# Wide hi products in the feed-forward: one matmul of 512 columns in place of two of 256

## The chip, the core and the metric

The kernel runs on one core of a Trainium2 chip. The metric is device time in microseconds (us) of one execution. Before the change the median of three runs is 1216.08 us (1213.23 to 1216.94).

## The reference: what is computed

A trunk of two layers on one sequence of 256 tokens with 1024 features, all in float32. Each layer has three sub-layers: a SwiGLU feed-forward, a token mixer, and a second feed-forward. So there are four feed-forwards. Layer 0 mixes by sparse attention beside a gated delta rule, layer 1 by latent attention. Every sub-layer modulates its input by the conditioning vector c and ends in a residual and a LayerNorm:

```python
def swiglu(u, w_gate, w_up, w_down):
    return (jax.nn.silu(u @ w_gate) * (u @ w_up)) @ w_down

def adaln_sublayer(x, m, f, ln_g, ln_b):
    shift, scale, gate = m[:, None, 0], m[:, None, 1], m[:, None, 2]
    y = f(x * (1 + scale) + shift)
    return layer_norm(DEEPNORM_ALPHA * x + (1 + gate) * y, ln_g, ln_b)
```

The inner width of a feed-forward is 2816. The modulation m is c (after a SiLU) times a matrix of 1024 rows per sub-layer, plus a bias.

## The kernel before, in words

**Products in three parts.** To reach float32 accuracy with the matmul type f32r, each operand is split into a hi part (rounded, a cast on ScalarE, ACT) and a lo part (the rest, a subtraction on VectorE, DVE, or on GpSimd, POOL): `split`, lines 257 to 259. A product of two split operands is three matmuls into the same PSUM bank: hi by hi, hi by lo, lo by hi (`mm3`, lines 261 to 266). TensorE (PE) loads the first operand as weights and streams the second as moving columns.

**A feed-forward** (`ffn`, line 412) goes over 22 tiles of 128 inner columns, in 11 chunks of two tiles. The input u stands transposed in `uT` [128, 2 (hi, lo), 8 row tiles, 256 tokens]. For each chunk the kernel loads and splits 256 columns of w_gate and w_up (`load`, line 439; the split tiles are named g and u, three buffers each) and the rows of w_down (`load_down`, line 456; tile hd). Each chunk but the first then fills four PSUM banks, gate and up of two tiles: for each of the 8 row tiles k an `mm3` with the weights hl[:, 0, k], hl[:, 1, k] and moving columns u[:, 0, k] (hi) or u[:, 1, k] (lo), 256 columns each (lines 529 to 535). So a bank takes 24 matmuls and uses 256 of its 512 columns. The tag `gu` has four banks, and the modulation sums use the same tag.

Behind each pair of banks ACT takes Silu of the gate bank into the tile sg (line 548), DVE multiplies the up bank by sg (line 551), and the result h is split (ACT, then DVE, line 553). The products with w_down follow one chunk later: for every tile four `mm3` with 512 moving columns into four banks of tag `acc` (`down`, lines 429 to 435, called at line 567); the last five tiles come at the end, bank by bank (lines 568 to 570).

The first chunk differs: in the first feed-forward it follows an order written by hand (lines 496 to 499), in the three others it is computed by rows of tokens (`by_rows`, line 463; `turned`, line 476).

**Beside it** runs the modulation of later sub-layers: `pace` (line 55) is called for each tile and takes steps of `mod_gen`, each of which loads 128 rows of a matrix (tile wd) and adds them, scaled, to macc on DVE (line 225). When eight steps are done, PE sums macc over its partitions, by four matmuls with ones in two halves (line 180) or by eight transposes (line 138); these stand in PE's queue behind the products of a chunk. In the first feed-forward the set-up of masks and positions runs beside the chunks as well.

**Order.** The engines run their queues in order. The tile framework writes the queues and the semaphores; `behind(mark)` has what is traced inside it come behind the marked instruction on its engine. `load(c)` of a chunk is behind the split of h of chunk c - 2 (line 522). SP's queue issues the loads in their order and waits where a buffer is not free: three buffers w8 for gate and up, three wd for w_down and the modulation. Memory pools of one sub-layer take over the space of the one before, and tiles there wait for the old ones.

Of the kernel before, what the change touches and what calls it, by code (L numbers as in the profile page):

```python
# [15 lines left out]
ALU = mybir.AluOpType  # L16
# [14 lines left out]
HYBRID_LATE, LATENT_LATE = (1,), (5,)  # of these rows, the second block's products come last  # L31


class Trunk:
# [20 lines left out]
    def pace(self, part):  # L55
        """runs the modulation up to its share of what this sub-layer takes of it"""
        goal = self.base + math.ceil((self.goal - self.base) * min(part, 1.0))
        while self.count < goal:
            self.count += next(self.bg)
        if part > 1.0:  # L60
            self.need(self.si, 2)
            if self.si + 1 < len(self.subs):
                self.need(self.si + 1, 0)

# [18 lines left out]
    def setup_bias(self):  # L83
        """the biases of shift and scale, as columns"""
# [25 lines left out]
    def behind(self, *marks):  # L110
        """what is traced here is issued behind the marked instructions of the same engines"""
# [9 lines left out]
    def warm(self, a):  # L121
        """keeps the PE array's clock up while nothing else can run on it"""
# [3 lines left out]
    def preload(self, func, after):  # L126
        """has the table of an activation function loaded behind what makes the tile after"""
        self.nc.scalar.activation(self.tl(self.const, [P, 1], "d"), after[:, 0:1], func)

# [1 line left out]
    def mod_cols(self, acc):  # L131
        """sum of acc over its partitions, [column % 128, column // 128]"""
# [9 lines left out]
    def mod_cols0(self, acc, c, use=None):  # L142
        """the same by products with c, which start earlier; use: takes two columns at a time"""
# [31 lines left out]
    def mod_gate(self, si, acc, G):  # L175
        """G holds the bias"""
# [8 lines left out]
    def mod_gen(self):  # L185
        """(c @ mod_w + mod_b) of every sub-layer, in the order of use; partition sums come last; yields tiles loaded"""
# [82 lines left out]
    def make_u(self, si, n, blocks):  # L269
        """n [P, NB, D] tokens on partitions -> uT = n * A + B, hi and lo [P, 2, KD, S]; blocks: one or all of them"""  # L270
# [57 lines left out]
    def residual(self):  # L328
        """x <- alpha * (n * g + b), in place of n; in four steps"""
# [16 lines left out]
    def epilogue(self, si, acc, last):  # L346
        """x holds alpha * x; acc the four banks of f(u); leaves the normalised rows in x, or the output."""
# [63 lines left out]
    def ffn(self, l, f, first):  # L411
        """first: the tiles of w_gate and w_up come first in the pool's memory, or those of w_down"""
# [6 lines left out]
        with ExitStack() as es:  # L419
# [18 lines left out]

            def load(c, tok):
# [23 lines left out]
            def by_rows(hls):  # L463
                """h of two tiles of columns, with tokens on partitions first: a block can run without the other"""
# [11 lines left out]
            def turned(pts):  # L476
                """the rest of by_rows"""
# [16 lines left out]
            else:  # L494
                # the products of the first chunk as their parts come: 0 hi hi, 1 hi lo, 2 lo hi; a pair of rows; gate, up
# [24 lines left out]
            for c in range(NC):  # L520
# [6 lines left out]
                else:  # L527
                    pts = {(s, g): self.bank("gu", (P, S)) for s in r2 for g in r2}
                    if c:
                        for s in r2:  # L530
                            for g in r2:
                                for k in range(KD):
                                    hl = hls[s, g]
                                    self.mm3(pts[s, g], hl[:, 0, k], hl[:, 1, k], u[:, 0, k], u[:, 1, k],
                                             k == 0, k == KD - 1)
# [8 lines left out]
                for s in r2:  # L544
                    i = 2 * c + s
                    if not tok:
                        sg = self.tl(hp, [P, S], "sg", bufs=2)
                        nc.scalar.activation(sg, pts[s, 0], AF.Silu)  # L548
                        if i == NT - 1 and f == 0:
                            self.preload(AF.Tanh, sg)  # L550
                        nc.vector.tensor_tensor(out=sg, in0=pts[s, 1], in1=sg, op=ALU.mult)
# [86 lines left out]
    def setup_rope(self):  # L638
        """cos and signed sin of the rotary angles: [frequency, token] and [token, frequency]"""
# [22 lines left out]
        # rows: 0-63 one, 64-95 cos, 96-127 signed sin  # L662
# [12 lines left out]
    def proj_t(self, pool, w, c0, n, use, engs=(None,)):  # L675
        """u @ w[:, c0 + o : c0 + o + 128] for o = 0, 128, ... < n, transposed: [columns, tokens]."""
# [17 lines left out]
    def tok_load(self, pool, w, c0, W):  # L694
        """the rows of w[:, c0 : c0 + W], split, in tiles of as many as fit"""
# [11 lines left out]
    def proj_tok(self, hls, W, by_block):  # L707
        """u @ the rows hls, with tokens on partitions; a bank for each block; by_block: one block after the other"""
# [17 lines left out]
    def attend(self, pool, q, k, v, bias, escale, po, i, sums, tags):  # L726
        """one head: q, k transposed, v [P, NB, 64]; exp(escale * (logits + bias) - max) @ v into po[:, :, i], its sums
        into sums[:, :, i]"""
# [21 lines left out]
    def attended(self, pool, po, sums, mix, k0):  # L750
        """divides the four heads of po by their sums; transposed into rows k0, k0 + 1 of mix"""
# [751 lines left out]
```

## Time and profile before

| what | us |
|---|---|
| three runs | 1213.23, 1216.08, 1216.94 |
| span of the profiled execution (first to last instruction) | 1212.3 |
| its own time beside the span | not listed; the runs are 0.9 to 4.6 longer than this span |
| busy PE, DVE, ACT, POOL | 1135.4, 905.5, 547.6, 255.4 |

The page of the profile gives busy time and instruction counts of each engine; groups of instructions by line, operation and tile; the waits between engines; and the instructions in order of time. PE's durations overlap, since matmuls are pipelined: the distance between two start times is the price of a matmul, not its duration. PEld is the weight load, beside PE. The four feed-forwards' chunks of two tiles start at about 46, 492, 694 and 1024 us.

### The profile page before, as it was taken

Reading aid. Unit: us, or ns where it says so; the run is one execution under the profiler, and the core shown is the slowest. Engines: PE = TensorE matmul, PEld = TensorE weight load, DVE = VectorE, ACT = ScalarE, POOL = GpSimd, SP = SyncE. Lnnn points to the kernel's source line nnn. Section 1 sums busy time; section 2 is a strip of 40 time slices with the busy share of each in tenths; the row PEclk is TensorE's granted clock in tenths of the full one; section 3 lists DMA queues with packets and bytes.
Section 4 is the critical chain, followed back from the end, with each engine's and each line's share of the span. In section 5 each row is a group of like instructions: output and inputs, shape, how many; then the busy total and the mean of one; then the engine's idle time right before and its main releaser. Section 6 shows DMA issues by size and latency. Waiting matters only on the chain.

```text
span 1212.3 us, 19687 instructions
## 1 busy us (share of the span) xinstructions
PE 1135.4 (94%) x7783; PEld 1035.5 (85%) x7783; DVE 905.5 (75%) x1376; ACT 547.6 (45%) x959; POOL 255.4 (21%) x186
## 2 busy tenths in 40 slices
PE   4998999999899998999999899899989998999997
PEld 3897999788787887989999889799978878899995
DVE  6699777698985677878885888778788438866545
ACT  0644444456433445533543543334456556544430
POOL 0631000224731452320000322000221234300001
PEclk9999999999999999999999999999999998999999
DMA  9779999454310586788997488889725135876620
GB/s 352 249 260 345 303 319 303 145 165 123 98 36 5 188 274 212 243 291 297 325 307 238 139 283 284 269 297 302 266 79 168 66 105 180 295 250 189 215 72 35
DMA packets 155334, 259.76 MB, mean 214 GB/s; under 512 B 8813, under 2 KB 117354, under 8 KB 155242
## 3 DMA queue, kind: packets, MB, share of 16 engines
q1 hardware_dynamic: 155050, 258.45, 63.9%
q8 instruction: 61, 1.00, 0.3%
q14 instruction: 31, 0.25, 0.1%
q10 hardware_dynamic: 192, 0.05, 0.0%
HBM read 257.43 MB, written 1.05 MB: 213 GB/s over the span
## 4 chain that ended last, share of the span: by engine, by line
PE 51%; DVE 22%; DMA 13%; ACT 5%; issue 5%; POOL 3%; SPq 0%; POOLq 0%; DVEq 0%; ACTq 0%
PE gu L265 8%; PE gu L264 8%; PE gu L263 7%; DMA wd<-ffn_w_down 7%; PE acc L265 6%; PE acc L263 6%; PE acc L264 6%; DVE macc L225 3%; DMA wd<-mod_w 3%; DMA w<-ffn_w_up 2%; DVE g L259 2%; POOL hd L259 2%; PE gu L732 2%; DVE u L259 2%; ACT hd L258 1%
## 5 line engine op out<-in xcount | busy, mean ns | idle before, releaser
L225 DVE SCALAR_TENSOR_TENSOR macc<-wd,csT,macc 128x1024 f32<-128x1024 f32 x112 | 169.0, 1509 | 27.1 <-DMA wd<-mod_w 26.5
L263 PE MATMUL gu<-uT,g 128*128 128x256 f32 x640 | 181.1, 283 | 1.4 <-ACT sg L548 1.4
L265 PE MATMUL gu<-uT,g 128*128 128x256 f32 x640 | 181.2, 283 | 1.2 <-DVE g L259 1.2
L265 PE MATMUL gu<-uT,u 128*128 128x256 f32 x640 | 181.2, 283 | 1.0 <-DVE u L259 1.0
L263 PE MATMUL gu<-uT,u 128*128 128x256 f32 x640 | 181.1, 283 | 0.0
L264 PE MATMUL gu<-uT,u 128*128 128x256 f32 x640 | 181.1, 283 | 0.0
L264 PE MATMUL gu<-uT,g 128*128 128x256 f32 x640 | 181.1, 283 | 0.0
L258 ACT CAST hd<-wd 128x1024 fp32r<-128x1024 f32 x88 | 92.2, 1049 | 136.8 <-DMA wd<-ffn_w_down 118.9
L263 PE MATMUL acc<-hd,h 128*128 128x512 f32 x352 | 141.3, 401 | 1.5 <-ACT h L258 1.5
L265 PE MATMUL acc<-hd,h 128*128 128x512 f32 x352 | 137.6, 391 | 1.1 <-DVE h L259 1.1
L264 PE MATMUL acc<-hd,h 128*128 128x512 f32 x352 | 137.7, 391 | 0.0
L259 DVE TENSOR_TENSOR g<-w,g 128x1024 fp32r<-128x1024 f32 x86 | 118.9, 1386 | 22.8 <-ACT g L258 22.3
L263 PEld LDWEIGHTS gu<-uT,g 128*128 128x128 f32 x640 | 122.7, 192 | 3.2 <-ACT sg L548 1.8
L265 PEld LDWEIGHTS gu<-uT,g 128*128 128x128 f32 x640 | 122.7, 192 | 1.6 <-DVE g L259 1.6
L264 PEld LDWEIGHTS gu<-uT,g 128*128 128x128 f32 x640 | 122.7, 192 | 1.4
L265 PEld LDWEIGHTS gu<-uT,u 128*128 128x128 f32 x640 | 122.9, 192 | 1.2 <-DVE u L259 1.2
L263 PEld LDWEIGHTS gu<-uT,u 128*128 128x128 f32 x640 | 122.9, 192 | 0.0
L264 PEld LDWEIGHTS gu<-uT,u 128*128 128x128 f32 x640 | 122.9, 192 | 0.0
L259 DVE TENSOR_TENSOR u<-w,u 128x1024 fp32r<-128x1024 f32 x81 | 104.1, 1290 | 24.5 <-ACT u L258 24.3
L258 ACT CAST u<-w 128x1024 fp32r<-128x1024 f32 (+1 forms) x89 | 91.6, 1039 | 62.7 <-DMA w<-ffn_w_up 51.9
L259 POOL TENSOR_TENSOR hd<-wd,hd 128x1024 fp32r<-128x1024 f32 x32 | 86.6, 2712 | 141.6 <-ACT hd L258 141.6
L259 POOL TENSOR_TENSOR hl<-w,hl 128x1024 fp32r<-128x1024 f32 x28 | 72.5, 2602 | 202.2 <-ACT hl L258 201.7
(392 smaller groups left out, 2495.2 us busy)
## 6 DMA issues: line engine op xcount, KB each, us to landing
wd<-mod_w SPq DMA_DIRECT2D x130, 512.0 KB, 4.8
wd<-ffn_w_down SPq DMA_DIRECT2D x88, 512.0 KB, 4.6
w<-ffn_w_gate SPq DMA_DIRECT2D x43, 1024.0 KB, 8.3
w<-ffn_w_up SPq DMA_DIRECT2D x43, 1024.0 KB, 6.9
w<-hyb_w_in SPq DMA_DIRECT2D x16, 1024.0 KB, 6.1
w<-mod_w SPq DMA_DIRECT2D x7, 1024.0 KB, 7.5
w<-hyb_w_out SPq DMA_DIRECT2D x4, 1024.0 KB, 4.9
w<-mla_w_out SPq DMA_DIRECT2D x4, 1024.0 KB, 5.4
```

Source lines behind the costliest of these rows:

```text
L225: step = nc.vector.scalar_tensor_tensor(acc, w, c, acc, ALU.mult, ALU.add)
L258: i = self.nc.scalar.copy(hi, src)
L259: return i, (eng or self.nc.vector).tensor_tensor(out=lo, in0=src, in1=hi.bitcast(F32), op=ALU.subtract)
L263: nc.tensor.matmul(out, lh, rh, start=first, stop=False)
L264: nc.tensor.matmul(out, lh, rl, start=False, stop=False)
L265: self.last_mm = nc.tensor.matmul(out, ll, rh, start=False, stop=last)
L732: nc.tensor.matmul(pt[:, b * S : (b + 1) * S], q[:, b * P : (b + 1) * P], k, start=True, stop=True)
```

## The change

In each chunk but the first, a bank holds [2, 256] columns. For each row tile the products of the hi weights with u-hi and u-lo become one matmul with 512 moving columns, u-hi's sum in the first half and u-lo's in the second. All eight of these come first; the eight products of the lo weights with u-hi then add into the first half. The two halves are added behind it: ACT copies the second half to SBUF, DVE adds the first half to it. Silu and the product of gate and up then read the sums in SBUF. The up sums have a new tile su of two buffers.

```diff
+    def mm_wide(self, out, hl, u):
+
+        nc = self.nc
+        for k in range(KD):
+            nc.tensor.matmul(out.rearrange("p a b -> p (a b)"), hl[:, 0, k], u[:, :, k], start=k == 0, stop=False)
+        for k in range(KD):
+            nc.tensor.matmul(out[:, 0], hl[:, 1, k], u[:, 0, k], start=False, stop=k == KD - 1)
...
+            def whole(pt, out):
+
+                nc.scalar.copy(out, pt[:, 1])
+                nc.vector.tensor_tensor(out=out, in0=pt[:, 0], in1=out, op=ALU.add)
+                return out
...
-                    pts = {(s, g): self.bank("gu", (P, S)) for s in r2 for g in r2}
+                    pts = {(s, g): self.bank("gu", (P, 2, S) if c else (P, S)) for s in r2 for g in r2}
                     if c:
                         for s in r2:
                             for g in r2:
-                                for k in range(KD):
-                                    hl = hls[s, g]
-                                    self.mm3(pts[s, g], hl[:, 0, k], hl[:, 1, k], u[:, 0, k], u[:, 1, k],
-                                             k == 0, k == KD - 1)
+                                self.mm_wide(pts[s, g], hls[s, g], u)
...
                         sg = self.tl(hp, [P, S], "sg", bufs=2)
-                        nc.scalar.activation(sg, pts[s, 0], AF.Silu)
+                        pg, pu = pts[s, 0], pts[s, 1]
+                        if c:
+                            pg, pu = whole(pg, sg), whole(pu, self.tl(hp, [P, S], "su", bufs=2))
+                        nc.scalar.activation(sg, pg, AF.Silu)
                         if i == NT - 1 and f == 0:
                             self.preload(AF.Tanh, sg)
-                        nc.vector.tensor_tensor(out=sg, in0=pts[s, 1], in1=sg, op=ALU.mult)
+                        nc.vector.tensor_tensor(out=sg, in0=pu, in1=sg, op=ALU.mult)
```

## Rows read from the trace of the kernel before

**Rows 1.** The page's part 1: span, busy time of each engine, share, instructions.

```profile
span 1212.3 us, 19687 instructions
PE 1135.4 (94%) x7783; PEld 1035.5 (85%) x7783; DVE 905.5 (75%) x1376; ACT 547.6 (45%) x959; POOL 255.4 (21%) x186
```

**Rows 2.** The page's groups, first and last of six: count, busy, mean ns, idle.

```profile
L263 PE MATMUL gu<-uT,g 128*128 128x256 f32 x640 | 181.1, 283 | 1.4 <-ACT sg L548 1.4
...
L264 PE MATMUL gu<-uT,g 128*128 128x256 f32 x640 | 181.1, 283 | 0.0
```

**Rows 3.** Timeline of PE, 599.8 to 604.2 us: start, duration, instruction.

```profile
599.87 0.39 PE L263 MATMUL acc<-hd,h 128*128 128x512 f32 x1
...
601.23 0.28 PE L263 MATMUL gu<-uT,g 128*128 128x256 f32 x1
...
604.11 0.28 PE L263 MATMUL gu<-uT,u 128*128 128x256 f32 x1
```

**Rows 4.** Busy time by stretch, late parts: stretch, length, engines, clock, DMA share, GB/s.

```profile
125.00:237.00 112.00, 110.19 (x769) 102.98 (x768) 82.80 (x107) 46.59 (x66) 6.00 (x4) 1.00 0.80 265
570.00:667.00 97.00, 97.00 (x690) 91.09 (x689) 72.87 (x90) 41.89 (x59) 1.24 (x1) 1.00 0.86 292
766.00:875.00 109.00, 109.00 (x750) 101.40 (x749) 84.71 (x103) 43.91 (x64) 3.63 (x2) 0.99 0.85 283
```

The busy times in these rows are of PE, PEld, DVE, ACT and POOL, in this order.

**Rows 5.** The same view, stretches in the opening of the feed-forwards.

```profile
60.00:99.00 39.00, 33.78 (x239) 31.54 (x237) 37.94 (x62) 13.74 (x18) 15.65 (x40) 1.00 0.83 277
487.00:511.00 24.00, 22.90 (x171) 21.78 (x171) 23.69 (x23) 13.35 (x20) 8.12 (x3) 1.00 0.72 246
511.00:570.00 59.00, 56.95 (x395) 52.41 (x394) 44.00 (x45) 23.56 (x33) 11.99 (x5) 1.00 0.88 293
550.00:560.00 10.00, 9.56 (x80) 9.39 (x80) 9.46 (x12) 4.47 (x6) 0.00 (x0) 1.00 0.91 305
687.00:714.00 27.00, 25.35 (x192) 23.92 (x191) 26.07 (x27) 15.35 (x23) 8.07 (x3) 1.00 0.65 216
1020.00:1038.00 18.00, 17.43 (x141) 16.71 (x139) 17.45 (x11) 12.83 (x17) 11.97 (x5) 1.00 0.71 230
```

**Rows 6.** Timeline of PE: instructions that waited, in brackets how long and for what.

```profile
98.99 1.17 PE L180 MATMUL gu<-macc,one 128*128 128x512 f32 x1 [4.19 <-DVE macc L225]
...
559.90 0.30 PE L138 MATMUL gu<-ident,macc 128*128 128x128 f32 x1 [0.44 <-DVE macc L225]
...
761.49 0.33 PE L138 MATMUL gu<-ident,macc 128*128 128x128 f32 x1 [0.90 <-ACT sg L548]
...
765.16 0.47 PE L138 MATMUL gu<-ident,macc 128*128 128x128 f32 x1 [3.01 <-DVE sg L551]
...
1038.75 0.50 PE L265 MATMUL acc<-hd,h 128*128 128x512 f32 x1 [1.07 <-DVE h L259]
```

**Rows 7.** Waits of PE, whole span: for whom, us in total, times, longest.

```profile
PE gu L282 <- DVE x L407: 6.0, 2, 3.6
...
PE gu L265 <- DVE g L259: 1.2, 1, 1.2
...
PE gu L265 <- DVE u L259: 1.0, 1, 1.0
```

**Rows 8.** Instructions on tile gu: ns min/median/max, first and last start, form.

```profile
L548 ACT ACTIVATE sg<-gu x82: 365/379/402, 40.6 to 1185.3; 128x256 f32<-128x256 f32 x82
L551 DVE TENSOR_TENSOR sg<-gu,sg x82: 407/419/427, 42.3 to 1188.2; 128x256 f32<-128x256 f32 x82
```

**Rows 9.** Timeline of DVE around 99 us.

```profile
98.76 0.42 DVE L551 TENSOR_TENSOR sg<-gu,sg 128x256 f32<-128x256 f32 x1
99.09 0.42 DVE L634 TENSOR_TENSOR nd<-nd,mneg 128x256 f32<-128x256 f32 x1
```

**Rows 10.** Busy time, sum over 46:99, 487:560, 687:762 and 1020:1039 us.

```profile
sum 220.00, PE 207.32 PEld 195.71 DVE 188.05 ACT 99.94 POOL 76.54; mean PE 51.83 PEld 48.93 DVE 47.01 ACT 24.98 POOL 19.13
```

**Rows 11.** Timeline of DVE in the second feed-forward, at 552 us.

```profile
552.18 0.42 DVE L259 TENSOR_TENSOR h<-sg,h 128x256 fp32r<-128x256 f32 x1 [0.47 <-ACT h L258]
```

## The prediction, made before the run

> **What bounds the kernel now.** I read the busy times first, then stretches, then the waits. The page's first part [rows 1] shows TensorE (PE) busy for 94% of the span, VectorE (DVE) 75%, ScalarE (ACT) 45%: PE is the engine to shorten, but the change pays for it on DVE, so DVE is the engine to watch. The cost groups [rows 2] show the six groups that the change touches: 640 matmuls each, 3840 in all, 40 chunks of 96 (ten chunks in each of four feed-forwards). Their 283 ns is a modelled duration that overlaps the next one, so the price is read from start times [rows 3]: six products with 512 columns start between 599.87 and 601.23 us, 227 ns apart; then the 24 products of one gate bank, 256 columns each, take 601.23 to 604.11 us, 120 ns apart. In a feed-forward's later part PE does not pause [rows 4]: in 570 to 667 us it is busy 97.00 of 97.00 us and in 766 to 875 us 109.00 of 109.00, with DVE at 72.87 and 84.71. There every nanosecond off PE is time off the kernel. In the opening of each feed-forward it is the other way round [rows 5]: DVE is busy 37.94 of 39 us (60 to 99), 23.69 of 24 (487 to 511), 26.07 of 27 (687 to 714) and 17.45 of 18 (1020 to 1038), and PE waits there for what DVE delivers. The places where it does are few [rows 6]: the first product of a modulation sum, which stands in PE's queue behind a chunk's products, waits 4.19 us at 98.99, 0.44 at 559.90, 0.90 and 3.01 at 761.49 and 765.16; and a lo product waits 1.07 for h at 1038.75. I call these the pins: what PE saves between the feed-forward's start and its last pin only makes the wait at the pin longer.
>
> **The change, part by part.** *Products.* In a bank 16 of the 24 products of 256 columns become 8 of 512. Before: 24 x 120 = 2880 ns. After: 8 x 227 + 8 x 120 = 2776 ns. That is 104 ns a bank, 0.416 us a chunk, and 160 banks give 16.6 us. The trace has no 512-column product whose moving operand lies in two runs (u-hi and u-lo are apart in memory). Bounds: 227 ns, the contiguous 512 [rows 3], and 240 ns, twice the 256, where nothing is saved; I take 227, the row with the same count of columns. The streaming itself is not shortened, only the part of each pitch that does not grow with the columns: 2 x 120 - 227 = 13 ns per pair.
>
> The Trainium skill, "TensorE: Matmul & The Clock Gate", section "Back-to-back issue gap", gives a warm gap of columns / 2.4 GHz plus 2.5 ns. An estimate from it would save 2.5 ns a pair, 3.2 us in 1280 pairs. The rows here disagree with it by some 11 ns at either width, so the sum above stays.
>
> *Order of the products.* The eight hi products now come first, so a bank can start when ACT's cast of its weights has ended, and DVE's subtraction (the lo part) is needed 8 x 0.227 = 1.8 us later. The two waits of PE for that subtraction, 1.2 and 1.0 us [rows 7], should go. Both lie ahead of the pin at 98.99, so what they free is late there instead: I count nothing.
>
> *ACT.* 160 copies of 128x256 out of PSUM; the nearest row is the Silu from the same kind of bank, 379 ns [rows 8]: 61 us in all. In the late stretches ACT is busy 46.59 of 112 us [rows 4], so the work itself costs nothing. The copy of the up half waits for PE to finish that bank, and the next weights' casts and the Silu are queued behind it; ACT already holds there today, since its next step, the cast of h, waits for DVE's product, which waits for the same bank. Without that cover it would cost its own 0.38 us.
>
> *DVE.* 160 additions of 128x256, one operand in PSUM; the row is the product of gate and up, the same form, 419 ns [rows 8], and where nothing holds it the next one starts 0.33 us after it [rows 9]. That is 4 x 0.42 = 1.7 us a chunk, 67 us in all. In 570 to 667 us there are 97 / 17.0 = 5.7 chunks (17.0 us is 96 x 0.120 + 24 x 0.227), so DVE goes from 72.87 to 82.5 of 97 us: hidden [rows 4]. In the full stretches it is not hidden, and I price the shift at the last pin of each feed-forward at 0.33 us an addition:
> - First, pin at 98.99: eight additions lie ahead of it in the full stretch (two of chunk 1, four of chunk 2, two of chunk 3): 2.7 us. The gain of chunks 1 to 3, 1.2 us, is lost in the wait. Together 3.9.
> - Second, pin at 559.90: DVE is busy 9.46 of the 10 us before [rows 5], with the two additions of chunk 4's first tile in them: 0.7, and the gain of chunks 1 to 4 lost, 1.7: 2.4. The additions of the chunks before fall into DVE's idle time (44.00 busy of 59 us from 511 to 570 [rows 5]).
> - Third, pins at 761.49 and 765.16: a gate bank is now freed by DVE's addition, not by ACT's Silu, and DVE stands in a run of weights there: 0.7, and 1.7 lost: 2.4.
> - Fourth, pin at 1038.75: four additions, 1.3, and 0.4 lost: 1.7.
>
> Bounds of this part: below, 5.0 us (the lost gain alone, 1.2 + 1.7 + 1.7 + 0.4, all additions behind the pins); above, every addition ahead of a pin at 419 ns plus the copy that it waits for, which is the second rival.
>
> *PSUM banks and memory.* The four banks are the same size. A bank is freed one ACT copy and one DVE addition after its last product, 0.8 us plus queueing; it is written again after the other three banks and 24 products of 512 columns, 3 x 2.8 + 5.4 = 13.8 us later: nothing, except at the pins counted above. The new tile su takes 2 KB of each partition, so pools of the next sub-layers lie elsewhere and may wait for other tiles. Bounds: 0 and 3.6 us, the longest wait of PE at such a border today (for the normalised rows, L407) [rows 7]; I take 0, as no row shows a wait on memory there.
>
> **The sum.** 16.6 - (3.9 + 2.4 + 2.4 + 1.7) = 16.6 - 10.4 = 6.2 us less. The profiled execution has a span of 1212.3 us [rows 1], 3.8 under the median of the runs, 1216.08; the saving is taken from the span and carried to the median: 1206.1 and **1209.9 us**.
>
> **The rivals.** (1) *The additions are free.* DVE's queue puts them where it waits for loads, and since PE frees buffers sooner, the loads that feed the pins come sooner too: 16.6 us, 1199.5. For it: DVE has 25% idle over the span [rows 1] and the lo parts gain 1.8 us of leeway. Against: at 60 to 99 us there is 1.06 us idle for eight additions. Chance 0.18.
>
> (2) *DVE becomes the bound, slower.* The place is DVE's in-order queue between a feed-forward's start and its last pin. Each addition there holds the queue until ACT's copy has ended, 0.38 + 0.42 = 0.80 us a bank, 3.2 a chunk; up to the pins there are 3 + 4 + 4 + 1 = 12 chunks, 38.4 us. It shows as PE idle where DVE is full, 39 + 24 + 10 + 27 + 18 = 118 us [rows 5] of the 220 us up to the pins [rows 10], 54%: 20.6 us. After the pins 28 chunks gain 11.6. Net 9.0 slower, 1225.1. It decides where an addition is put ahead of a weight split whose PE consumer is waiting; for it, DVE waits 0.47 us for ACT's cast of h today, the same kind of hold [rows 11]. Against: the next weights' splits can be queued between copy and addition. Chance 0.18.
>
> (3) *The wide product saves nothing*, at 240 ns because of its two runs: then only the additions at the pins count, 2.7 + 0.7 + 0.7 + 1.3 = 5.4 slower, 1221.5. Chance 0.07. The gap rule of the Trainium skill's page "TensorE: Matmul & The Clock Gate" ("Back-to-back issue gap") lies near this case; the 120 and 227 ns of this trace speak against it.
>
> (4) *The memory moves.* Borders cost up to 3.6 us; at one or two of three borders the gain of 6.2 is mostly gone: about 1215. Chance 0.12.
>
> **How the numbers follow.** A measurement of this kernel can tell about 0.3%, 3.6 us, from no change. The forecast has 0.45, of which 0.33 is faster by more than that and 0.12 within it. Rival 1 is faster (0.18). Rival 2 gives 0.16 slower and 0.02 same, rival 3 0.04 slower and 0.03 same, rival 4 0.02 faster, 0.07 same, 0.03 slower. Together 0.53 faster, 0.24 same, 0.23 slower. The forecast's own range is 1204 to 1214 (11.6 less, if all additions fall behind the pins, to about 2 less); the range for 8 in 10 takes in most of rival 1 below and rivals 3 and 4 above: 1200 to 1222.
>
> **What would show it.** Start times in the late part of a feed-forward: eight products 227 ns apart, then eight 120 apart, a bank in 2.78 us; if the eight are 240 apart, rival 3. The DVE group of additions: 160 of about 0.42 us, ACT copies about 0.38. Idle PE before the gate sum near 99 us: about 8 us, not 4.2; unchanged means rival 1, over 12 rival 2. The stretch from the last pin to a feed-forward's end shorter by 2.5 us in the second and third, by 3.7 in the fourth. The prediction is wrong if PE pauses in those late stretches, or if DVE there passes 95%.

## The result, and the profile after: slower by 1.1%

The changed kernel took 1228.75 us (median of 4 runs, 1224.46 to 1231.6), the kernel before, on the same chip, 1215.45 (4 runs): ratio 1.0113, 95% interval 1.0093 to 1.0133. That is 13.3 us slower, where 6.2 us faster was forecast, and it lies above the forecast's 1200 to 1222. The profiled execution took 1231.19 us with a span of 1229.3, 2.4 above its median.

The page's part 1 of the changed kernel answers to [rows 1]:

```profile
span 1229.3 us, 17343 instructions
PE 1129.4 (92%) x6503; PEld 969.7 (79%) x6503; DVE 961.2 (78%) x1536; ACT 595.3 (48%) x1119; POOL 257.5 (21%) x186
```

1280 matmuls are gone, and 160 DVE additions and 160 ACT copies came. The instructions of the lines of copies (L449) and additions (L450), with ns min/median/max, first and last start and form, then PE's timeline in the later part of the second feed-forward (start, duration, instruction; runs of equal matmuls are one row):

```profile
L449 ACT COPY su<-gu x80: 351/356/374, 52.3 to 1205.1; 128x256 f32<-128x256 f32 x80
...
L450 DVE TENSOR_TENSOR su<-gu,su x80: 408/417/426, 52.7 to 1205.5; 128x256 f32<-128x256 f32 x80
```

```profile
605.68 1.98 PE L272 MATMUL gu<-uT,g 128*128 128x512 f32 x8
607.50 1.12 PE L274 MATMUL gu<-uT,g 128*128 128x256 f32 x8
608.45 2.00 PE L272 MATMUL gu<-uT,u 128*128 128x512 f32 x8
```

A bank goes from 605.68 to 608.45, 2.77 us (forecast 2.78), and the eight wide products take 1.82, 227 ns each: two runs of moving columns cost the same as one contiguous 512 [rows 3]. The copies and additions have the forecast sizes. So the pieces are right, and the time went elsewhere. PE's longest waits, whole span (for whom, us in total, times, longest), answer to [rows 7]:

```profile
PE gu L290 <- DVE x L415: 16.4, 4, 8.6
...
PE gu L180 <- DVE macc L225: 8.8, 2, 7.9
PE acc L263 <- ACT h L258: 7.8, 6, 2.5
PE gu L138 <- DVE su L450: 5.9, 3, 5.0
PE acc L265 <- DVE h L259: 4.7, 3, 1.8
```

The first row was 6.0 in all, 3.6 at most [rows 7]; the waits for h are new in this size. To see where time is lost I take the start of the same matmul (the products of h with w_down, and the transposes of x at a border) in two traces and subtract. Us against the profiled execution of before, spans as profiled; "tile n" is the n-th tile of h, from 0; the labelled kernels come in the next section:

| place (time before) | after | e1 | e17 | e12 | e18 |
|---|---|---|---|---|---|
| first feed-forward, tile 5 (105.2) | +2.6 | 0.0 | +0.5 | +1.8 | -0.7 |
| its tile 17 (220.8) | 0.0 | -2.6 | -2.1 | -0.8 | -0.7 |
| its end (234.6) | +5.9 | -2.6 | -2.1 | -0.7 | -0.7 |
| second, tile 7 (564.6) | +5.2 | -4.2 | -0.2 | +0.6 | -0.8 |
| its tile 17 (663.6) | +4.3 | -6.4 | -1.9 | -0.6 | -0.8 |
| its end (677.4) | +8.7 | -6.4 | -1.9 | +3.5 | -0.8 |
| third, tile 7 (769.8) | +8.6 | -11.7 | -6.2 | +4.8 | -1.3 |
| its tile 17 (868.8) | +7.1 | -13.7 | -0.9 | +2.6 | -1.3 |
| its end (882.6) | +9.2 | -13.7 | -0.9 | +3.7 | +0.2 |
| next border, first transpose (884.4) | +16.0 | -14.1 | -1.9 | +1.9 | +0.4 |
| fourth, tile 1 (1040.9) | +20.6 | -12.9 | -2.0 | +3.9 | +0.6 |
| its tile 17 (1189.2) | +17.0 | -16.3 | -4.9 | +0.3 | -3.0 |
| end of the span (1212.3) | +17.0 | -16.3 | -4.9 | +0.3 | -3.0 |

In the column "after" two steady parts gain as forecast (first feed-forward 2.6 from tile 5 to 17, fourth 3.6 from tile 1 to 17), and two gain less (second and third 0.9 and 1.5 from tile 7 to 17, where five chunks would give 2.1). What is lost is lost in three kinds of places: the ends of the first three feed-forwards (5.9, 4.4 and 2.1 us), the border before the latent attention (6.8), and that attention itself (+16.0 to about +20, 4). The late stretches, by length and busy time of PE, PEld, DVE, ACT, POOL, clock, DMA share, GB/s, answer to [rows 4]:

```profile
126.00:237.00 111.00, 107.29 (x563) 91.83 (x562) 88.92 (x127) 51.72 (x86) 5.69 (x4) 0.98 0.81 274
575.00:674.00 99.00, 95.81 (x507) 81.24 (x506) 81.88 (x111) 49.40 (x83) 3.10 (x2) 1.00 0.84 285
```

PE, which never paused in the second of these before, is now idle 3.2 us of it, with DVE at 83%: not a full engine, but a late one. At the end of the first feed-forward DVE's timeline shows how (in brackets the idle time ahead of an instruction and what ended it):

```profile
216.28 0.42 DVE L450 TENSOR_TENSOR sg<-gu,sg 128x256 f32<-128x256 f32 x1
220.40 2.67 DVE L225 SCALAR_TENSOR_TENSOR macc<-wd,csT,macc 128x1024 f32<-128x1024 f32 x2 [3.71 <-DMA wd<-mod_w]
222.99 0.42 DVE L450 TENSOR_TENSOR su<-gu,su 128x256 f32<-128x256 f32 x1
223.40 1.28 DVE L225 SCALAR_TENSOR_TENSOR macc<-wd,csT,macc 128x1024 f32<-128x1024 f32 x1
224.60 0.42 DVE L565 TENSOR_TENSOR sg<-su,sg 128x256 f32<-128x256 f32 x1
...
227.68 0.43 DVE L259 TENSOR_TENSOR h<-sg,h 128x256 fp32r<-128x256 f32 x1 [0.47 <-ACT h L258]
```

ACT's copy for the addition at 222.99 began at 217.05 and took 0.35. The addition stands in the queue behind modulation steps that wait 3.71 us for their load. In the kernel before, the same steps wait 2.27 us for their load and start at 214.07, and PE does not pause; here they start at 220.40, half of h's way (copy, addition, Silu, product, copy, subtraction) lies behind them, and no products of a further chunk are left for PE. PE waits 2.48 and 1.23 us for h, and from 228.0 to 231.3 it is granted 0.50 (1.2 GHz, the lower of its two levels), about 1.7 more.

At the border before the latent attention the order of DVE's queue is another one. Before, the splits of that attention's weights (tile big) stand between the epilogue's steps (tmp, x); after, they stand behind at least nine of them. DVE's timeline, of the kernel before and then of the changed one (part):

```profile
871.99 1.79 DVE L259 TENSOR_TENSOR big<-w,big 128x672 fp32r<-128x672 f32 x1 [0.42 <-ACT big L258]
873.69 0.68 DVE L381 SCALAR_TENSOR_TENSOR tmp<-acc,G 128x512 f32<-128x512 f32 x1
874.29 1.69 DVE L259 TENSOR_TENSOR big<-w,big 128x672 fp32r<-128x672 f32 x1
```

```profile
890.03 0.69 DVE L392 BATCH_NORM_STATS2 st<-x 128x6 f32<-128x512 f32 x1
890.64 2.38 DVE L259 TENSOR_TENSOR big<-w,big 128x672 fp32r<-128x672 f32 x3
896.35 0.86 DVE L259 TENSOR_TENSOR big<-w,big 128x672 fp32r<-128x672 f32 x1 [3.33 <-ACT big L258]
```

So a buffer of raw weights comes free late, and SP issues the fourth load into it at 891.55 instead of 873.08, 18.5 us later, of which 9.2 are the shift of the feed-forward's end. POOL's split of that load comes next, and the reciprocal root of the normalisation (L118, L119) stands behind it; before, that split was done earlier, and the root waited for DVE's mean and variance (mv). SP, POOL and PE in three timelines, first of the kernel before, then of the changed one:

```profile
873.08 0.38 SPq L1333 DMA_DIRECT2D w<-mla_w_in  x1
...
882.63 0.22 POOL L118 TENSOR_SCALAR rs<-mv 128x1 f32<-128x1 f32 x1 [2.38 <-DVE mv L386]
...
884.39 1.15 PE L282 MATMUL gu<-ident,x 128*128 128x128 f32 x8 [1.81 <-ACT x L405]
```

```profile
891.55 0.38 SPq L1347 DMA_DIRECT2D w<-mla_w_in  x1
...
897.05 1.62 POOL L259 TENSOR_TENSOR big<-w,big 128x672 fp32r<-128x672 f32 x1 [9.85 <-ACT big L258]
898.64 0.22 POOL L118 TENSOR_SCALAR rs<-mv 128x1 f32<-128x1 f32 x1
...
900.39 1.97 PE L290 MATMUL gu<-ident,x 128*128 128x128 f32 x8 [8.61 <-DVE x L415]
```

PE's wait at this border was 1.81 us and is 8.61, which is the 6.8 lost there. None of these steps waits for an addition. In the attention behind it, PE's own queue has another order too (between two groups of products of the tile dg, seven products of cT with big instead of six), and PE is granted 0.50 from 900.4 to 903.7 and from 955.0 to 958.3, where before it had 1.00 in 870 to 890 and in 930 to 950; an estimate of half of these 6.6 us gives 3.3 of the 4 lost there. What could reorder these queues is the memory of the one new tile, su.

### The profile page after: what moved, and what is told of

Same layout as the page of the kernel before. It is cut to its first block, busy times and chain, and to the rows that moved or that the text cites. A ratio compares the mean times of both kernels' runs of the same rounds, so it can differ in the third digit from the quotient of the medians.

```text
span 1229.3 us, 17343 instructions
## 1 busy us (share of the span) xinstructions
PE 1129.4 (92%) x6503; PEld 969.7 (79%) x6503; DVE 961.2 (78%) x1536; ACT 595.3 (48%) x1119; POOL 257.5 (21%) x186
## 4 chain that ended last, share of the span: by engine, by line
PE 35%; DVE 31%; DMA 19%; ACT 7%; issue 5%; POOL 2%; SPq 0%; POOLq 0%; DVEq 0%; ACTq 0%
DMA wd<-ffn_w_down 10%; PE gu L272 7%; DVE macc L225 5%; PE acc L265 5%; PE acc L263 5%; PE acc L264 5%; DMA wd<-mod_w 4%; PE gu L274 4%; DVE u L259 3%; DVE g L259 3%; DVE hd L259 2%; ACT hd L258 2%; PE gu L746 2%; DMA w<-ffn_w_up 2%; DMA w<-mod_w 1%
## 5 line engine op out<-in xcount | busy, mean ns | idle before, releaser
L225 DVE SCALAR_TENSOR_TENSOR macc<-wd,csT,macc 128x1024 f32<-128x1024 f32 x112 | 167.8, 1498 | 21.9 <-DMA wd<-mod_w 21.2
L272 PE MATMUL gu<-uT,u 128*128 128x512 f32 x640 | 160.5, 393 | 1.1 <-ACT u L258 1.1
L272 PE MATMUL gu<-uT,g 128*128 128x512 f32 x640 | 160.1, 392 | 1.1 <-DVE su L450 0.7
L272 PEld LDWEIGHTS gu<-uT,g 128*128 128x128 f32 x640 | 117.1, 188 | 24.1 <-DVE su L450 0.9
L272 PEld LDWEIGHTS gu<-uT,u 128*128 128x128 f32 x640 | 115.1, 189 | 22.0 <-ACT u L258 1.3
L258 ACT CAST u<-w 128x1024 fp32r<-128x1024 f32 (+1 forms) x89 | 92.0, 1039 | 41.4 <-DMA w<-ffn_w_up 41.3
L258 ACT CAST g<-w 128x1024 fp32r<-128x1024 f32 (+1 forms) x89 | 92.1, 1038 | 13.9 <-DMA w<-ffn_w_gate 11.0
L259 DVE TENSOR_TENSOR hd<-wd,hd 128x1024 fp32r<-128x1024 f32 x56 | 70.2, 1259 | 31.0 <-ACT hd L258 31.0
L258 ACT CAST h<-sg 128x256 fp32r<-128x256 f32 x82 | 33.3, 406 | 124.7 <-DVE sg L565 124.6
L274 PEld LDWEIGHTS gu<-uT,g 128*128 128x128 f32 x640 | 87.2, 190 | 6.7 <-DVE g L259 0.5
L274 PEld LDWEIGHTS gu<-uT,u 128*128 128x128 f32 x640 | 87.3, 190 | 6.3
L274 PE MATMUL gu<-uT,g 128*128 128x256 f32 x640 | 89.3, 282 | 0.1
L274 PE MATMUL gu<-uT,u 128*128 128x256 f32 x640 | 89.2, 282 | 0.0
L263 PEld LDWEIGHTS acc<-hd,h 128*128 128x128 f32 x352 | 67.6, 192 | 26.6 <-ACT h L258 10.4
```

The costliest lines, as they stand in the source:

```text
L225: step = nc.vector.scalar_tensor_tensor(acc, w, c, acc, ALU.mult, ALU.add)
L258: i = self.nc.scalar.copy(hi, src)
L259: return i, (eng or self.nc.vector).tensor_tensor(out=lo, in0=src, in1=hi.bitcast(F32), op=ALU.subtract)
L263: nc.tensor.matmul(out, lh, rh, start=first, stop=False)
L272: nc.tensor.matmul(out.rearrange("p a b -> p (a b)"), hl[:, 0, k], u[:, :, k], start=k == 0, stop=False)
L274: nc.tensor.matmul(out[:, 0], hl[:, 1, k], u[:, 0, k], start=False, stop=k == KD - 1)
```

## The experiments

The times are medians (lowest to highest, number of runs); the next column is the difference from the kernel before on the same chip in the same comparison, the last the ratio with its interval.

| kernel | us | against before | ratio |
|---|---|---|---|
| the change | 1228.75 (1224.46-1231.6, 4) | +13.3 | 1.0113 [1.0093, 1.0133] |
| e1 products only | 1199.94 (1197.82-1204.63, 4) | -15.9 | 0.989 [0.9853, 0.9926] |
| e2 additions only | 1236.61 (1235.47-1237.49, 4) | +20.8 | 1.0186 [1.0155, 1.0217] |
| e4 last chunk narrow | 1219.04 (1215.16-1223.07, 10) | +3.2 | 1.0037 [1.0016, 1.0058] |
| e6 border order | 1220.52 (1217.06-1227.03, 10) | +4.7 | 1.005 [1.0027, 1.0073] |
| e10 e1 with tile su | 1207.92 (1205.35-1216.02, 9) | -6.9 | 0.996 [0.994, 0.9979] |
| e12 su beside tag v | 1214.16 (1211.91-1218.25, 10) | -0.6 | 1.0008 [0.9993, 1.0023] |
| e13 e4 with e12 | 1212.04 (1208.09-1213.64, 10) | -2.8 | 0.9978 [0.9964, 0.9991] |
| e14 middle chunks wide | 1212.96 (1207.99-1216.98, 12) | -1.8 | 0.9988 [0.9973, 1.0003] |
| e15 additions on POOL | 1230.48 (1226.37-1236.53, 4) | +15.6 | 1.0128 [1.009, 1.0167] |
| e16 modulation behind | 1216.71 (1211.71-1220.72, 10) | +1.8 | 1.0017 [0.9998, 1.0037] |
| e17 load off the chain | 1210.86 (1208.79-1215.58, 10) | -4.1 | 0.9964 [0.9948, 0.9979] |
| e18 wide in the last only | 1210.12 (1208.63-1211.05, 6) | -4.8 | 0.9954 [0.9938, 0.9969] |

**e1, e2: each half of the change alone.** e1 makes the wide products but leaves the second halves (weights-hi with u-lo) out of the result; e2 adds halves that 24 narrow products make.

```diff
 e1
-pg, pu = whole(pg, sg), whole(pu, self.tl(hp, [P, S], "su", bufs=2))
+pg, pu = pg[:, 0], pu[:, 0]
 e2, in mm_wide
-nc.tensor.matmul(out.rearrange("p a b -> p (a b)"), hl[:, 0, k], u[:, :, k], start=k == 0, stop=False)
+nc.tensor.matmul(out[:, 0], hl[:, 0, k], u[:, 0, k], start=k == 0, stop=False)
+nc.tensor.matmul(out[:, 1], hl[:, 0, k], u[:, 1, k], start=False, stop=False)
```

> Wide products as in the change, but the second halves are not added: Silu and the product of gate and up read the first half of each bank, so the products of hi weights with u-lo are left out of the result; ACT copies and DVE additions are gone. Theory A (the ends of the feed-forwards and the border before latent attention eat the gain, through the additions): PE gains 0.416 us a chunk and only what stands before the openings' waits is lost, so 11.6 us less than before, 1204, at best 1199; eight products 227 ns apart as in the changed kernel. Rival B (any work added to DVE slows it, wherever it stands): the same here, about 1204. Rival C (the wide products themselves, or their order, disturb the queues): 1215 or more.

> The 24 narrow products in the order of before, but those of hi weights with u-lo go to the second half of the bank, and the halves are added as in the change: the cost of the additions without the gain on PE. Theory A: the changed kernel without its gain behind the openings, 1228.75 + 11.6 = 1240; the four late stretches last as long as before, the three ends of feed-forwards that have other DVE work wait 2 to 6 us each, the border before latent attention 7 us. Rival B: also about 1240, but with PE pausing in the late stretches too. Rival C: near before, 1215 to 1220.

e1 keeps 15.9 of the 16.6 us, more than the 11.6 that was expected: the products are what the timeline says. The column e1 of the first table shows more. Only the pin of the first feed-forward holds (0.0 at tile 5); in the second and third the pins move up with PE (-4.2 at tile 7 of the second, -11.7 in the third). Earlier buffers and so earlier loads would explain that; it was not tested. The additions with their copies and the tile su cost 20.8 us without the wide products, and the wide products give back 7.9 beside them (1236.61 - 1228.75), half of what they give without.

**e6, e10, e12: the border and the memory of su.** e6 forces one step of the old order: the epilogue's first DVE step before the latent attention is put behind the third split of big. e10 is e1, with Silu writing into a tile su of the same size and place and no instruction more. e12 is the whole change with su taken from the three buffers of tag v, which exist already.

```diff
 e6, in epilogue; T.first_v is the split of rows 4 of mla_w_in
-after = []
+after = [self.first_v] if self.subs[si] == (1, 0) else []
 e10, on e1
+sg2, sg = sg, self.tl(hp, [P, S], "su", bufs=2)
...
-nc.vector.tensor_tensor(out=sg, in0=pu, in1=sg, op=ALU.mult)
+nc.vector.tensor_tensor(out=sg2 if c else sg, in0=pu, in1=sg, op=ALU.mult)
+sg = sg2 if c else sg
 e12
-whole(pu, self.tl(hp, [P, S], "su", bufs=2))
+whole(pu, self.tl(self.wp, [P, S], "v", bufs=3))
```

> The changed kernel, with the first DVE step of the epilogue before latent attention put behind the third split of that layer's input weights, as it stood in the kernel before. Theory A: the fourth load of those weights is issued when the weights' buffer is free, some 18 us earlier, and the wait of PE for the normalised rows there falls from 8.6 to about 2 us: 7 us less than the changed kernel, 1221.5 to 1222. Rival B (DVE's load as such): the wait only moves, at most 2 us less, 1227.

> As the run with wide products and no additions (1199.9; the products of hi weights with u-lo are left out of the result), but Silu writes into the new tile su of two buffers in the feed-forward's pool, so that the pool is 2 KB larger as in the change; no instruction more. In its queue on DVE the splits of latent attention's input weights stand behind the epilogue's steps, as in the changed kernel. Theory M (the place of su in memory moves the pools and with them the order at the border and in latent attention): 6 to 8 us lost at the border and about 4 in latent attention, 1210 to 1212. Rival N (the additions' time in the queues causes both): 1200, as without su.

> The changed kernel, complete, with su in the three buffers of 1 KB that the epilogue uses for its input's tiles (tag v), so that no pool grows. The splits stand ahead of the epilogue on DVE again. Theory M: the wait at the border before latent attention (7 us) and the 4 us in latent attention go, the ends of the feed-forwards still lose 5 to 12: 1228.75 - 11 = 1218. Rival N: 1226 or more.

e6 brings 8.2 us back (1228.75 to 1220.52); its trace loses 1.1 at the border instead of 6.8, and still about 4 in the attention behind it. In e10 no addition exists, and the time rises by 9.0 against e1 (-6.9 instead of -15.9; 1210 to 1212 was expected); the border's queue turns over as in the changed kernel, and its trace loses 6.5 at that border, where e1's loses nothing. DVE's timeline there, of e1 and then of e10:

```profile
859.80 0.68 DVE L389 SCALAR_TENSOR_TENSOR tmp<-acc,G 128x512 f32<-128x512 f32 x1
860.40 1.69 DVE L259 TENSOR_TENSOR big<-w,big 128x672 fp32r<-128x672 f32 x1
```

```profile
873.87 0.69 DVE L392 BATCH_NORM_STATS2 st<-x 128x6 f32<-128x512 f32 x1
874.48 2.38 DVE L259 TENSOR_TENSOR big<-w,big 128x672 fp32r<-128x672 f32 x3
880.09 0.86 DVE L259 TENSOR_TENSOR big<-w,big 128x672 fp32r<-128x672 f32 x1 [3.23 <-ACT big L258]
```

e12 has every instruction of the change and restores the old order; it is 13.9 us better than the change (-0.6 instead of +13.3). So the place of one 2 KB tile is the largest single cost, and the additions' time in the queue is not what turned the border over. All the traces agree: the five kernels with su in the feed-forward's pool (the change, e2, e4, e6, e10) have the new order of PE's products in the attention, and the nine others, before among them, the old one; at the border DVE's order goes the same way, but for e6, which forces one step of it back. (e12 also has three buffers for su instead of two; e10 turns the order over with two.) How the place comes to decide the order of the queues stays open. In the first table the changed kernel and e12 end 16.7 us apart: 8.6 of it at the border, 2.6 in the attention and 5.8 at the first feed-forward's end. That end lost 5.9 in the changed kernel's trace and 1.0 in e6's with the same code there: in e6 the steps that wait for their load start at 216.62, not 220.40. So it differs between executions.

**e4, e13, e14, e16: the ends.** e4 makes the last chunk of each feed-forward as before the change, e13 does the same on e12; e14 on e12 is wide only for the middle chunks (4 to 9 in the first, 2 to 9 in the second and third, 2 to 10 in the fourth). e16 on e12 puts the modulation's DVE steps of the last chunk behind its split of h.

```diff
 e4, e13: the wide form, its banks and the additions
-if c:
+if 0 < c < NC - 1:
 e14
+lo, hi = 4 if first == "start" else 2, NC if l and f else NC - 1
-if c:
+if lo <= c < hi:
 e16
-with self.behind(*[part] if c == 1 else after):
+with self.behind(*[part] if c in (1, NC - 1) else after):
```

> The changed kernel with the last chunk of each feed-forward in the old form (24 narrow products, no additions): one tenth of the additions and of the gain undone. The order at the border before latent attention stays that of the changed kernel. Theory A: the waits at the ends of the first three feed-forwards (5.9, 4.4 and 2.1 us) go, 1.7 us of gain go with them: 1228.75 - 12.4 + 1.7 = 1218. Rival B: a tenth of the loss of 13.3 + 11.6 us goes, less 1.7: about 1228.

> Both: the last chunk of each feed-forward narrow and su in the buffers v. Theories A and M together: 1219.0 of the run with the last chunk narrow, less 6.5 at the border and 4 in latent attention, 1208.5: faster than before by 7. Rivals B and N: 1217 or more.

> A version meant to be faster than both: wide chunks only where PE is the bound, chunk 4 to 9 of the first feed-forward, 2 to 9 of the second and third, 2 to 10 of the fourth; su in the buffers v. 31 chunks x 0.416 = 12.9 us, of which the gain before the second and third feed-forward's pins (chunks 2 to 4, twice 1.2) is lost: 10.4 less than before, 1205. Rival B: the additions cost DVE time in every chunk, no less than the last-chunk-narrow version with su in v.

> e12 (the complete change with su beside the tiles of tag v, 1214.16 us) and one edit: in the last chunk of a feed-forward the modulation's steps on DVE are put behind the split of h, as they already are in the second chunk. Theory of the ends (the last chunk's addition stands in DVE's queue behind modulation steps that wait for their transfers): the loss across the end of the second feed-forward, 4.1 us in e12, falls under 1, and the time to 1209 to 1212, about e13's. Theory of the chain (the copy and the addition themselves make the end longer, some 0.9 us a tile): the loss stays at 2 us or more and the time within 2 us of e12's.

e4 is 9.7 us faster than the change although it gives up four chunks' gain (4 x 0.416 = 1.7): the ends cost nothing in its trace, the border keeps its 6.5. On e12 the same edit gives 2.1 (e13, which was expected at 1208.5). e14 missed: 1212.96 where 1205 was expected, with runs spread over 9 us. e16 missed too: the second feed-forward's end still loses 3.9 us, and the time is no better than e12's (1216.71 and 1214.16), so at that end modulation steps are not the cause. What is, stands in the timelines of DVE and POOL. First the kernel before, DVE and then POOL; then the changed one, with PE's wait as the last line:

```profile
664.20 1.22 DVE L259 TENSOR_TENSOR g<-w,g 128x1024 fp32r<-128x1024 f32 x1
665.33 0.42 DVE L259 TENSOR_TENSOR h<-sg,h 128x256 fp32r<-128x256 f32 x1
...
665.76 5.75 POOL L259 TENSOR_TENSOR u<-w,u 128x1024 fp32r<-128x1024 f32 x2 [116.78 <-DVE h L259]
```

```profile
669.91 1.23 DVE L259 TENSOR_TENSOR g<-w,g 128x1024 fp32r<-128x1024 f32 x1
671.16 2.48 DVE L259 TENSOR_TENSOR h<-sg,h 128x256 fp32r<-128x256 f32 x1
...
670.90 4.99 POOL L259 TENSOR_TENSOR u<-w,u 128x1024 fp32r<-128x1024 f32 x2 [117.39 <-ACT u L258]
...
673.70 0.50 PE L265 MATMUL acc<-hd,h 128*128 128x512 f32 x1 [1.78 <-DVE h L259]
```

The last split of h, 128x256, takes 0.42 us where it ends before POOL's pair begins, and 2.48 where POOL was first by 0.26: it ends at 673.64, 0.28 behind the first of POOL's two splits (673.36). Behind a copy and an addition it comes second: in the change, e12 and e16 it took 2.48, in before, e1, e13 and e18 0.42. PE waits 0.41 and 1.78 us there, and then runs 3.4 us at the lower clock level (granted 0.50, 1.2 GHz), having been busy 2.03 of the 4 us before. The stretches 671 to 675 and 675.1 to 678.5 us of the changed kernel:

```profile
671.00:675.00 4.00, 2.03 (x8) 1.38 (x9) 3.38 (x4) 2.02 (x3) 4.00 (x2) 1.00 0.01 4
675.10:678.50 3.40, 3.40 (x10) 2.63 (x9) 3.17 (x3) 0.00 (x0) 0.79 (x1) 0.50 0.16 14
```

Half a clock for 3.4 us is 1.7, an estimate; with the waits, 0.41 + 1.78 + 1.7 = 3.9 of the 4.4 lost at this end.

**e17, e15: what the additions cost away from these places.** e17 is e1 plus as many DVE additions of the second half, put behind the split of h and into a scratch tile that nothing reads; the result lacks the second halves as in e1. e15 is e13 with the additions on POOL: ACT copies both halves.

```diff
 e17, on e1
-pg, pu = pg[:, 0], pu[:, 0]
+off, pg, pu = (pg, pu), pg[:, 0], pu[:, 0]
...
+for o in off if c else ():
+    with self.behind(part):
+        nc.vector.tensor_tensor(out=self.tl(self.wp, [P, S], "v", bufs=3), in0=o[:, 1], in1=sg, op=ALU.add)
 e15, on e13, in whole
+half = self.tl(self.wp, [P, S], "v", bufs=3)
-nc.vector.tensor_tensor(out=out, in0=pt[:, 0], in1=out, op=ALU.add)
+nc.scalar.copy(half, pt[:, 0])
+nc.gpsimd.tensor_tensor(out=out, in0=half, in1=out, op=ALU.add)
```

> The products-only kernel (1199.94 us; the second halves, the products of the high weights with the low part of u, are left out of the result) with DVE's additions given back as load: as many additions of the second half in PSUM to the gate's tile, of the same size, but put behind the split of h and written to a scratch tile of tag v that nothing reads, with no ACT copy. Chain theory (the additions cost because h is late by them, at the openings and the ends): 1199 to 1203. Load theory (DVE's queue is what fills: everything behind the additions, modulation and epilogue, comes later wherever they stand): 1207 to 1213. The two PSUM banks are held longer here too, so between 1203 and 1207 neither is told apart.

> From e13 (last chunk of each feed-forward narrow, su beside the scratch tiles of tag v, 1212.04 us) the additions leave DVE: ACT copies both halves (about 0.4 us each) and POOL adds them (estimated 0.65 us, a quarter of its 128x1024 split's 2.4 us). Queue theory (what is still lost beside the products-only kernel's 1199.94 is the additions' time in DVE's queue, which also delays what stands behind it): DVE is as before, the time falls to 1203 to 1208, and the marks in the second feed-forward and at the border before the latent attention stand 3 us or more earlier than e13's. Any-step theory (each added step on the way from products to h costs, whichever engine has it): 1211 to 1216. POOL theory (POOL's own queue, with the splits of the up weights in it, is late): above 1216, with matmuls waiting for POOL.

e17 is 11.8 us worse than e1 (-4.1 instead of -15.9) though no addition stands on h's own way: the time falls to the load theory. PE's waits in e1, then in e17, show the place, the sums of the modulation (L180 and L138; L571 is the line of the off-chain additions):

```profile
PE gu L180 <- DVE macc L225: 3.7, 2, 2.7
...
PE gu L138 <- DVE sg L565: 2.8, 2, 1.6
```

```profile
PE gu L180 <- DVE v L571: 9.0, 3, 5.1
...
PE gu L180 <- DVE macc L225: 5.5, 1, 5.5
```

That is 14.5 us, and none before L138, against 6.5. But 9.0 of the 14.5 end with one of the added additions: the sums share the tag gu with the banks that these read and so hold longer. e17 therefore prices DVE's load and the longer hold of the PSUM banks together, and load alone is not shown. That 11.8 is near the prediction's 10.4 is in part luck: the two long waits of these 9.0 (3.60 at 523.9, 5.13 at 799.3) are at sums that it did not count as pins. e12, with the additions back on h's way and ACT's copies, is 3.5 above e17.

e15's POOL additions have a median of 742 ns for the up half, near the estimate of 0.65 us, and of 1005 for the gate half, and DVE waits for them. The instructions of POOL's line, then the longest group of DVE's waits:

```profile
L452 POOL TENSOR_TENSOR sg<-v,sg x72: 721/1005/5711, 53.3 to 1183.9; 128x256 f32<-128x256 f32 x72
L452 POOL TENSOR_TENSOR v<-v,v x72: 721/742/1819, 56.4 to 1186.7; 128x256 f32<-128x256 f32 x72
```

```profile
DVE sg L573 <- POOL v L452: 65.5, 42, 6.0
```

DVE's splits of h now mean 543 ns instead of e13's 461, and its products wait 65.5 us for POOL. At 1230.48 it is no way out. (ACT also has twice the copies; that was not separated.)

**e18: wide products where DVE has time to give.** Only the fourth feed-forward is wide; su lies beside tag v. Its expectation says that no modulation is left there. That is not quite so: 7 of DVE's modulation steps (L225) lie there, against 28, 29 and 34 in the first three, and DVE is busy for 70.35 of the 129 us from 1060 to 1189 in the kernel before.

```diff
+wide = c and l and f
...
-if c:
+if wide:
```

> The wide products in the fourth feed-forward alone, where no modulation is left for DVE (ten chunks; su beside the tiles of tag v); the first three feed-forwards as before the change. Load theory (the additions take DVE's time from the modulation, and where there is none the products' gain is kept): nothing moves up to the fourth feed-forward, its opening costs up to 1 us, and its ten chunks give 0.36 to 0.42 us each, so 3 to 4 us less than before, 1211 to 1212, no later than the complete change with su there (1214.16). Spread theory (the gain per chunk is eaten by whatever adds steps to a chunk, modulation or not): within 1 us of before, 1214 to 1216.

It gave 1210.12, 4.8 us less than before, somewhat more than expected, and in its trace -3.6 from tile 1 to tile 17 (+0.6 to -3.0), the forecast 0.4 a chunk. It uses a quarter of the wide products and is faster than the change by 18.6 us and than before by 0.5% (interval 0.3 to 0.6%): the best complete version here by its median.

## Why the prediction was wrong, step by step

- *Products*, 16.6 us: right. 227 ns and 2.77 us a bank; e1 keeps 15.9.
- *The pins*, 10.4 us: right at the first, where PE waits 7.95 us at 102.02 (forecast about 8); the rest of the reasoning did not hold. "The gain lost in the wait", 5.0, is no fixed loss: without the additions the pins of the second and third move up (e1). With the additions off h's way 11.8 us are lost (e17), partly at sums that were not on the list, so that the size agrees is in part luck.
- *DVE* after the pins, "hidden [rows 4]": this failed. I read 97 us of steady state and put no term for the last chunk, where no product of a next chunk covers h's way. The ends of the first three feed-forwards lost 5.9, 4.4 and 2.1 us in the changed kernel's trace and nothing in e4's. (The third can lose without an addition: e18, narrow there, lost 1.5.) The fourth, with no modulation step or next weights on DVE in its last chunk, lost nothing. So the stretch from the last pin (tile 7) to the end, forecast 2.5 shorter, was 3.5 longer in the second and 0.6 longer in the third; in the fourth it was 3.6 shorter (forecast 3.7). With the border out of the way e12's ends lose 0.1, 4.1 and 1.1 in its trace and e17's nothing, which may be the 3.5 us between their medians.
- *PSUM banks and memory*, "I take 0", at most 3.6: this failed most. The tile su cost 9.0 us without any addition (e10 against e1) and 13.9 with them (change against e12). The bound was the longest wait that a border shows today, and it was read at another border, that behind the latent attention (3.6 at 1007.4 before, 3.6 at 1027.2 after). At the border ahead of it the reordered queue moves a DMA issue by 9.3 us beyond the shift of the feed-forward's end and makes a wait of 8.6 where 1.8 was.
- The sum by runs, each against its own kernel before: -15.9 (e1), +11.8 (load and held banks, e17 - e1), +3.5 (on h's way, e12 - e17), +13.9 (su's place, change - e12) = +13.3. These are steps of one path; in another order the parts would differ, as su's place does (9.0 in e10).
- *ACT*, nothing: right as to its load, 48% busy, but its copies lie in h's way at the ends.
- *Rivals.* The first is out: the additions are not free, as the first pin's wait of 7.95 us shows; its 1199.5 is met by e1 (1199.94), which has none. The second forecast 1225.1, near the result for another reason: its mechanism, without su's place, gives -0.6 (e12) and not +9.0. The fourth had the mechanism and a third of its size. The third is out (227 ns). The gap rule that the prediction takes from the Trainium skill's page "TensorE: Matmul & The Clock Gate" ("Back-to-back issue gap") is given there for an isolated matmul, so it was no measure for this stream; the 120 and 227 ns of the trace decide. The wrong-if of the prediction held: PE pauses in the late stretches, with DVE at 83%, far from 95%.

## What to carry to other kernels

A saving on the busiest engine that is paid with steps on a second engine has to be priced at three places: in the steady part, at the pins, and in the last chunk, where nothing covers the longer way to its result; a steady-state window shows the first alone. A new tile in a pool is an edit of its own: let it use buffers that exist (here 13.9 us), and compare the order of the queues at the next border before pricing anything else. Then keep the change only where the second engine has time to give, as in e18.

## What the runs showed of the hardware that was not expected

- A DVE operation of 0.42 us took 2.48 when POOL had begun a 128x1024 split 0.26 us earlier, and POOL's pair of splits took 5.75 us where it began behind that operation and 4.99 where it began ahead. The Trainium skill, "Trainium Architecture — The Big Picture", "What this means for kernel authors", says that the two engines share a port pair under an exclusive lock; these rows agree (the 2.48 us end 0.28 behind POOL's first split). The Trainium skill's page "Perfetto Trace Analysis", "Optimizing Scalar/DVE Operations", says that moving work between those two might not help; e15 agrees (1230.48 us against e13's 1212.04, with ACT's copies doubled).
- A moving operand in two runs costs as much as a contiguous one: 227 ns at 512 columns.
- The same code at the first feed-forward's end cost 5.9 us in one profiled execution and 1.0 in another kernel's (e6), where a load let DVE go on at 216.62 and not at 220.40; and the changed kernel's runs spread over 7 us (1224.46 to 1231.6) where those of before spread over 3.7.
